# Recurrent mixer: the receptance's mixed tokens take the key's places tile by tile, and the systems leave by the inverse's places

## The chip, the cores and the metric

The kernel runs on one core of a Trainium2 chip as a single program. A core has a matrix engine (TensorE, in the rows PE, with its weight loads as PEld), a vector engine (VectorE, DVE), a scalar engine (ScalarE, ACT), a general engine (GpSimd, POOL) and a queue of transfers (SyncE, SP). Each works off its own list of instructions in order and waits for the others by semaphores. The metric is the device time of one execution in microseconds (us); the median of three runs before the change is 2302.98 us.

## The reference

Two layers, each a feed-forward network, a mixer, and a feed-forward network. The second mixer, which the change touches, is a recurrent one over 512 tokens with 16 heads of width 64:

```python
xx = jnp.pad(u, ((0, 0), (1, 0), (0, 0)))[:, :-1] - u

def proj(i):
    return (u + xx * mu[i]) @ w_in[:, int(offs[i]):int(offs[i + 1])]

r, k, v = proj(0), proj(1), proj(2)
...
def step(state, inp):
    r_t, w_t, k_t, v_t, kk_t, a_t = inp
    sa = jnp.einsum('bhvk,bhk->bhv', state, -kk_t)
    state = (state * w_t[:, :, None, :] + sa[..., None] * (kk_t * a_t)[:, :, None, :]
             + v_t[..., None] * k_t[:, :, None, :])
    return state, jnp.einsum('bhvk,bhk->bhv', state, r_t)
```

Receptance r, key k and value v are products of 1024 x 1024 with token-mixed copies of the input u. The recurrence is computed in chunks of 64 tokens; per head and chunk a triangular 64 x 64 system has to be inverted.

## The kernel before, in words

All of this is in `rwkv`. A product is done by `dense(i, off, evict, eng, ...)`: 8 tiles of 128 features, two halves g of four output banks each, and per tile and bank three matmuls of 128 x 512 (high and low parts of both operands, `mm3`, L195), so 192 for a product. In the first half the mixed tile `kt` is made by `mix` (L832 to L841): ScalarE scales u into a place of the tag `tb` (L837), VectorE adds the shifted u (L838), ScalarE rounds it to the high part in a place of the tag `big` (L839), and `eng` subtracts for the low part (L840). `tb` has two places, `big` eight, which is one product's tiles.

Around the products:

- `key` evicts the key's banks (L970 to L976: squares on ScalarE, a product with the decays, and the two sides A and B in the large tiles `ab`); its squares are summed by matmuls (L972).
- `root` (L982 to L984) makes the reciprocal norms, `normalise` spreads them by a matmul (L992) and VectorE scales A and B (L995). `systems(g, th)` multiplies B by A per head and chunk (L1010), VectorE masks the result (L1012) into a place of `tb`, and SyncE writes it to memory as md (L1013). g is the half of the heads, th the half of the chunks.
- `corners` (L1027, L1029) and `blocks(th)` (L1035 to L1045) read md back; `blocks` inverts 32 x 32 blocks by forward substitution on GpSimd: 31 steps of two dependent operations, 62 in all, in tiles of the tag `two`, which has four places. It carries a high priority. There is one inverse for each th.
- `receive` (L1094) folds r into A, `bonus` (L1102, L1104) sums r times k, `value` (L1117, L1119, L1120) parks v in memory.
- `convert` and `double` (L1059 to L1089) turn an inverse of 32 x 32 blocks into one of 64 x 64: a copy on ScalarE, transfers through memory (td), two rounds of 128 small matmuls (L1081, L1083) and evictions. The first is placed in the value's product, the second in the recurrence.
- `run` is the recurrence: 16 cycles u, in an order written out by hand. From cycle 1 on it multiplies by the first inverse (L1190), in each cycle GpSimd takes powers for the group norm (L1232) and products with the bonus (L1245), and VectorE scales by those powers one cycle later (L1235).

The order of instructions on each engine is set by a scheduler outside `run`: it takes instructions as they are written, moves them forward where they would be ready, and prefers those of high priority. On the chip each list is then fixed.

Of the kernel before, what the change touches and what calls it, by code (L numbers as in the profile page):

```python
# [9 lines left out]
F32 = mybir.dt.float32  # L10
# [6 lines left out]
P = 128  # L17
S = 512
# [14 lines left out]
C = 64  # L33
# [16 lines left out]
def weave(first, *others, every=1):  # L50

    for i, _ in enumerate(first):
        for g in others:
            if i % every == 0:
                next(g, None)
# [14 lines left out]
class Net:  # L70
# [711 lines left out]
    def rwkv(self, u, layer):  # L782
        nc, io = self.nc, self.io
# [48 lines left out]
        def mix(i, kt, eng):  # L832

            t = big()
            h, l = halves(t)
            x = vp.tile([P, S], F32, tag="tb", name="tb", bufs=2)
            nc.scalar.activation(x, u[:, kt, :], AF.Copy, scale=omu(i, kt))  # L837
            nc.vector.scalar_tensor_tensor(x[:, 1:], u[:, kt, 0:S - 1], mu(i, kt), x[:, 1:], op0=OP.mult, op1=OP.add)  # L838
            nc.scalar.activation(h, x, AF.Copy)  # L839
            eng.tensor_sub(l, x, h.bitcast(F32))  # L840
            return h, l  # L841
# [66 lines left out]
        def decays():  # L908

            kap = self.small([P, 2], "kap", 1)  # L910
            last = sides(KT - 1)[1][:, NC - 1, 2 * C - 1:]
            for i, k in enumerate((KAPPA, -KAPPA)):
                nc.vector.tensor_scalar(kap[:, i:i + 1], last, 0.0, k, op0=OP.mult, op1=OP.add)
                for g in gs:
                    n = g.shape[0]
                    nc.vector.scalar_tensor_tensor(kap[0:n, i:i + 1], g, 0.0, kap[0:n, i:i + 1], op0=OP.mult, op1=OP.add)
            for j in range(KT):
                A, B = sides(j)
                nc.scalar.activation(A[:, :, C:], v3(cums[j]), AF.Exp, scale=kap[:, 1:2])
                nc.scalar.activation(cums[j], cums[j], AF.Exp, scale=kap[:, 0:1])  # L920
                nc.scalar.activation(A[:, :, 0:C], B[:, :, C:], AF.Identity, scale=par(KA, j), bias=par(OKA, j))
                nc.gpsimd.tensor_copy(pc[:, j, :], A[:, :, 2 * C - 1])
                yield
# [6 lines left out]
                raws[n] = self.raw_weights()  # L930
            return raws.pop(n)

        def dense(i, off, evict, eng, other=iter(()), done=None):

            xs = {}
            for g in range(2):
                acc = [self.bank() for _ in range(4)]
                for kp in range(KT // 2):
                    w = self.weights(raw=load(off + 4 * g + kp))
                    anchor["act"], anchor["sp"] = self.last_hi, self.last_raw  # L940
                    for kk in range(2):
                        kt = 2 * kp + kk
                        if g == 0:
                            xs[kt] = mix(i, kt, eng())
                        for n in range(4):
                            ns, ws = slice(P * n, P * n + P), slice(512 * kk + P * n, 512 * kk + P * n + P)
                            if i == 2:
                                lhs, rhs = [t[:, ns] for t in xs[kt]], [t[:, 512 * kk:512 * kk + 512] for t in w[1:]]
                            else:
                                lhs, rhs = [t[:, ws] for t in w[1:]], xs[kt]  # L950
                            anchor["pe"] = self.mm3(acc[n], lhs, rhs, kt == 0, kt == KT - 1)
                        next(other, None)
                        yield
                for n in range(4):
                    evict(g, n, acc[n])
                    yield
                if done:
                    yield from done(g)
# [42 lines left out]
        def systems(g, th):  # L1001

            mask = tri[:, 0:C].rearrange("p (o t) -> p o t", o=1).to_broadcast([P, 2 * HC, C])
            for jp in range(2 * g, 2 * g + 2):
                gb = self.bank("ot").rearrange("p (q t) -> p q t", t=C)
                for q in range(2 * HC):
                    A, B = sides(2 * jp + q // HC)
                    c = HC * th + q % HC
                    for e in range(2):
                        nc.tensor.matmul(gb[own[e], q, :], B[own[e], c, 0:C], A[own[e], c, 0:C], start=True, stop=True)  # L1010
                gs = vp.tile([P, 2 * HC, C], F32, tag="tb", name="tb", bufs=2)
                nc.vector.tensor_tensor(gs, gb, mask, op=OP.mult)  # L1012
                nc.sync.dma_start(out=md[th][8 * jp:8 * jp + 8].rearrange("q e s t -> (e s) q t"), in_=gs)  # L1013
                yield
# [306 lines left out]
        def steps(*gs):  # L1321
            for g in gs:
                yield from g
# [11 lines left out]
                yield from normalise(0, 0, NC)  # L1335
                yield from steps(systems(0, 0), systems(0, 1))

        weave(steps(dense(1, 5, key, vec, decays(), heads_of)))
        for th in range(2):
            root(1, slice(HS * th, HS * th + HS))  # L1340
            weave(normalise(1, HC * th, HC))
            weave(systems(1, th))
            corners(th)
        weave(blocks(0))
        weave(blocks(1))
        weave(dense(0, 13, receive, vec))
        weave(bonus())
        fill = dense(2, 21, value, vec)
        for _ in range(9):
# [248 lines left out]
```

## Time and profile before

| what | us |
|---|---|
| median of three runs | 2302.98 (2302.13 to 2304.86) |
| the profiled execution | 2306.49 |
| its span, first to last instruction | 2304.6 |
| TensorE busy | 2190.6 (95%) |
| VectorE busy | 1527.2 (66%) |
| ScalarE busy | 1159.3 (50%) |
| GpSimd busy | 363.9 (16%) |

All later times are of the profiled execution, in us from the start of its span. Busy time counts what an engine executes; a busy TensorE is not one at its peak, since matmuls overlap, and its clock has two levels, shown as a share of the upper one. The recurrent mixer lies between about 1500 and 1930: the key's second half ends near 1603, the receptance's product runs from 1651 to the start of the value's, and the recurrence ends near 1860.

### The profile page before, as it was taken

To read this page: it belongs to the slowest core of one execution; us is meant where nothing else is said; L and a number is where in the kernel's file an instruction comes from. 1 tells how busy PE (TensorE), PEld (TensorE's weight loads), DVE (VectorE), ACT (ScalarE), POOL (GpSimd) and SP (SyncE) were. 2 spreads that over 40 slices of the span, in tenths; PEclk is the share of its full clock that TensorE was granted. 3 is DMA by queue.
4 is the path that set the end of the run, shared out by engine and by line. 5 is a ranking of instruction groups with operands and counts; after the bars stand their busy time and mean duration, and the time that the engine had idled before them with its cause. 6 is when DMAs were issued, how large, how long until landed. Compare 5 with 4: busy or idle time off the path is not lost.

```text
span 2304.6 us, 38449 instructions
## 1 busy us (share of the span) xinstructions
PE 2190.6 (95%) x15398; PEld 1921.0 (83%) x15398; DVE 1527.2 (66%) x2447; ACT 1159.3 (50%) x2282; POOL 363.9 (16%) x372
## 2 busy tenths in 40 slices
PE   7999999999999999999999999988699989899998
PEld 7999888877666889998799998866587867899987
DVE  8888625346777688872588874386663556888733
ACT  5555514465665455552445554286333754555532
POOL 4000004023100310000130000012493423100000
PEclk9999999999989999999999999999798989999999
DMA  4333333211001323333323333232443124333331
GB/s 174 101 104 111 101 95 109 83 46 46 29 1 65 101 83 110 107 94 102 110 83 100 103 101 108 85 104 92 75 114 122 47 83 162 94 109 99 96 107 67
DMA packets 93283, 214.33 MB, mean 93 GB/s; under 512 B 40752, under 2 KB 41392, under 8 KB 93104
## 3 DMA queue, kind: packets, MB, share of 16 engines
q1 hardware_dynamic: 93104, 211.88, 29.6%
q8 instruction: 121, 1.98, 0.4%
q14 instruction: 58, 0.48, 0.1%
HBM read 196.84 MB, written 15.01 MB: 92 GB/s over the span
## 4 chain that ended last, share of the span: by engine, by line
issue 29%; PE 24%; DVE 5%; POOL 4%; ACT 3%; DMA 1%; SPq 0%; DVEq 0%; POOLq 0%; ACTq 0%
PE p L195 19%; POOL two L1045 1%; POOL tmpi L1043 1%; PE p L1154 1%; ACT junk L218 1%; POOL sp L347 1%; PE p L1178 0%; DVE slot L201 0%; PE p L1170 0%; DVE xl L201 0%; DVE h L261 0%; PE p L972 0%; PE p L862 0%; PE p L1206 0%; PE p L1199 0%
## 5 line engine op out<-in xcount | busy, mean ns | idle before, releaser
L195 PE MATMUL p<-xh,whi 128*128 128x256 f32 (+1 forms) x1640 | 479.4, 296 | 18.3 <-ACT xh L200 8.4
L195 PE MATMUL p<-xl,whi 128*128 128x256 f32 (+1 forms) x1640 | 477.4, 294 | 3.4 <-DVE xl L201 3.4
L195 PE MATMUL p<-xh,wlo 128*128 128x256 f32 (+1 forms) x1640 | 457.9, 294 | 1.4 <-DVE wlo L201 1.4
L174 DVE TENSOR_TENSOR wlo<-raw,whi 128x1024 fp32r<-128x1024 f32 x150 | 190.2, 1269 | 316.7 <-ACT whi L170 316.7
L195 PE MATMUL p<-whi,slot 128*128 128x512 f32 x1280 | 395.1, 389 | 0.0
L195 PE MATMUL p<-slot,whi 128*128 128x256 f32 x1920 | 361.1, 284 | 12.5 <-issue 6.0
L170 ACT ACTIVATE whi<-raw 128x1024 fp32r<-128x1024 f32 x166 | 174.8, 1056 | 339.8 <-PE p L195 314.9
L195 PEld LDWEIGHTS p<-xh,whi 128*128 128x128 f32 x1640 | 319.1, 195 | 29.2 <-ACT xh L200 9.8
L195 PEld LDWEIGHTS p<-xl,whi 128*128 128x128 f32 x1640 | 320.2, 195 | 9.0 <-DVE xl L201 4.7
L195 PEld LDWEIGHTS p<-slot,whi 128*128 128x128 f32 x1920 | 303.4, 193 | 14.9 <-issue 6.2
L195 PEld LDWEIGHTS p<-xh,wlo 128*128 128x128 f32 x1640 | 309.5, 195 | 6.8 <-DVE wlo L201 1.6
L200 ACT ACTIVATE whi<-xn 128x1024 fp32r<-128x1024 f32 (+1 forms) x240 | 220.0, 917 | 184.7 <-PE p L195 133.8
L201 DVE TENSOR_TENSOR wlo<-xn,whi 128x1024 fp32r<-128x1024 f32 (+1 forms) x240 | 255.8, 1067 | 50.1 <-ACT whi L200 47.0
L195 PEld LDWEIGHTS p<-whi,slot 128*128 128x128 f32 x1280 | 240.0, 188 | 49.7
L195 PE MATMUL p<-slot,wlo 128*128 128x256 f32 x960 | 270.1, 284 | 0.0
L195 PE MATMUL p<-wlo,slot 128*128 128x512 f32 x640 | 249.0, 389 | 0.0
L222 POOL TENSOR_TENSOR rstd<-rstd,mhalf 128x1 f32<-128x1 f32 x48 | 30.1, 628 | 1348.0 <-DVE rstd L221 1347.2
L195 PEld LDWEIGHTS p<-slot,wlo 128*128 128x128 f32 x960 | 184.5, 193 | 0.0
L391 ACT ACTIVATE sp<-p 128x256 f32<-128x256 f32 x320 | 121.2, 379 | 112.6 <-PE p L195 112.6
L195 PEld LDWEIGHTS p<-wlo,slot 128*128 128x128 f32 x640 | 120.1, 188 | 24.9
L195 PE MATMUL p<-big,whi 128*128 128x512 f32 (+1 forms) x288 | 94.9, 412 | 12.0 <-ACT big L839 11.2
L200 ACT ACTIVATE whi<-raw 128x1024 fp32r<-128x1024 f32 x80 | 84.1, 1051 | 40.1 <-PE p L195 40.1
(321 smaller groups left out, 3754.1 us busy)
## 6 DMA issues: line engine op xcount, KB each, us to landing
raw<-in_wpack SPq DMA_DIRECT2D x252, 512.0 KB, 3.6
xn<-in_wpack SPq DMA_DIRECT2D x80, 512.0 KB, 3.5
hpark<-h SPq DMA_DIRECT2D x8, 512.0 KB, 2.7
h<-hpark SPq DMA_DIRECT2D x8, 512.0 KB, 4.7
h<-in_x SPq DMA_DIRECT2D x4, 512.0 KB, 7.1
gpost<-in_ffn_norm_post SPq DMA_DIRECT2D x4, 512.0 KB, 6.6
md<-tb SPq DMA_DIRECT2D x8, 256.0 KB, 2.8
td<-two SPq DMA_DIRECT2D x4, 512.0 KB, 2.8
```

The costliest lines, as they stand in the source:

```text
L170: self.last_hi = nc.scalar.activation(hi, raw, AF.Copy)
L174: (eng or nc.vector).tensor_sub(lo, raw, hi.bitcast(F32))
L195: m = self.nc.tensor.matmul(out, lhs[a], rhs[b], start=start and i == 0, stop=stop and i == 2, skip_group_check=more)
L200: i = self.nc.scalar.activation(hi, src, AF.Copy)
L201: return i, (eng or self.nc.vector).tensor_sub(lo, src, hi.bitcast(F32))
L218: nc.scalar.activation(self.junk(), src[q], AF.Square, scale=1.0 / (half * math.sqrt(D)), accum_out=ss[:, q:q + 1])
L222: nc.gpsimd.tensor_tensor(r[:, 1:2], r[:, 0:1], self.mhalf[:, 0:1], op=OP.pow)
L347: nc.gpsimd.tensor_sub(t4, q(xh, 1, 0, b), t2)
L391: copy = lambda dst, bank: nc.scalar.activation(dst, bank[:, 0:H], AF.Copy)
L1043: nc.gpsimd.tensor_tensor(t, ms[:, j, j + 1:32].rearrange("p (i o) -> p i o", o=1).to_broadcast([P, n, m]), T[:, j:j + 1, 0:m].to_broadcas ...
L1045: nc.gpsimd.tensor_tensor(T[:, j + 1:32, 0:m], T[:, j + 1:32, 0:m], t, op=OP.subtract)
L1154: nc.tensor.matmul(gb[e][:, j * P:j * P + P], B[own[e], j, c, :], A[own[e], j, c, :], start=True, stop=True)
```

## The change

Three edits. The receptance's mix of a tile is called right after the key's second half is done with the same tile (`then`), into the place of `big` that the key's tile leaves, and its subtraction goes to GpSimd instead of VectorE. The receptance's product no longer mixes; it takes the tiles that it is given. The masked systems are written from a place of `two` and no longer of `tb`, and the first inverse stands before the second half of the chunks' systems, so that each th is followed by its own inverse.

```diff
-        def dense(i, off, evict, eng, other=iter(()), done=None):
-
-            xs = {}
+        def dense(i, off, evict, eng, other=iter(()), done=None, xs=None, then=None):
+
+            xs = xs or {}
...
-                        if g == 0:
+                        if g == 0 and kt not in xs:
                             xs[kt] = mix(i, kt, eng())
...
                         next(other, None)
+                        if g and then:
+                            then(kt)
                         yield
...
-                gs = vp.tile([P, 2 * HC, C], F32, tag="tb", name="tb", bufs=2)
+                gs = two()[:, 0:S].rearrange("p (q t) -> p q t", t=C)
                 nc.vector.tensor_tensor(gs, gb, mask, op=OP.mult)
...
-        weave(steps(dense(1, 5, key, vec, decays(), heads_of)))
+        mixed = {}
+
+        def early(kt):
+
+            mixed[kt] = mix(0, kt, nc.gpsimd)
+
+        weave(steps(dense(1, 5, key, vec, decays(), heads_of, then=early)))
+        reads = dense(0, 13, receive, vec, xs=mixed)
         for th in range(2):
             root(1, slice(HS * th, HS * th + HS))
             weave(normalise(1, HC * th, HC))
             weave(systems(1, th))
             corners(th)
-        weave(blocks(0))
-        weave(blocks(1))
-        weave(dense(0, 13, receive, vec))
+            weave(blocks(th))
+        weave(reads)
         weave(bonus())
```

In the changed kernel the lines from L974 on are two further down: L992 becomes L994, L1010 L1012, L1012 L1014, L1043 L1045 and so on; the text below uses the old numbers except in the lists of the changed kernel.

TensorE before, after the key's product: p_16012 and p_16032 are the systems of the first chunks that the first inverse waits for, p_16082 and p_16102 those of the second chunks, p_16328 is the receptance's first bank.

```order
L992 MATMUL p_16008<-rinv,two 128x256
L1010 MATMUL p_16012<-ab 64x64 x16
L1010 MATMUL p_16032<-ab 64x64 x16
L992 MATMUL p_16066<-rinv,two 128x256
L992 MATMUL p_16070<-rinv,two 128x256
L992 MATMUL p_16074<-rinv,two 128x256
L992 MATMUL p_16078<-rinv,two 128x256
L1010 MATMUL p_16082<-ab 64x64 x16
L1010 MATMUL p_16102<-ab 64x64 x16
L195 MATMUL p_16328<-big,whi 128x512
L195 MATMUL p_16329<-big,whi 128x512
```

All systems stood ahead of the receptance. TensorE now, just after the key's last bank: p_16376 and p_16377 are the receptance's first two banks, L994 is the first half of heads being normalised.

```order
L195 MATMUL p_16377<-big,whi 128x512
L195 MATMUL p_16376<-big,wlo 128x512
L195 MATMUL p_16377<-big,wlo 128x512
L195 MATMUL p_16376<-big,whi 128x512 x2
L195 MATMUL p_16376<-big,wlo 128x512
L195 MATMUL p_16377<-big,whi 128x512 x2
L195 MATMUL p_16377<-big,wlo 128x512
L994 MATMUL p_15733<-rinv,two 128x512
L994 MATMUL p_15737<-rinv,two 128x512
L195 MATMUL p_16376<-big,whi 128x512
L195 MATMUL p_16377<-big,whi 128x512
```

The receptance starts before the first norm is spread and encloses these steps. TensorE now, in the value's first half (banks p_16689 to p_16692): p_16060 and p_16080 are the first chunks' systems, which before stood as p_16012 and p_16032.

```order
L195 MATMUL p_16691<-whi,big 128x512
L195 MATMUL p_16691<-wlo,big 128x512
L195 MATMUL p_16691<-whi,big 128x512
L1012 MATMUL p_16060<-ab 64x64 x16
L1012 MATMUL p_16080<-ab 64x64 x16
L195 MATMUL p_16692<-whi,big 128x512
L195 MATMUL p_16692<-wlo,big 128x512
```

The systems that open the first inverse have moved behind all 192 matmuls of the receptance and 18 of the value. GpSimd before, from the key's last eviction to the first inverse (L1043, L1045):

```order
L974 TENSOR_TENSOR ab<-tmp,ab 128x8x64 x2
L1029 MEMSET xl 32x16x32 x2
L974 TENSOR_TENSOR ab<-tmp,ab 128x8x64 x2
L1029 MEMSET xl 32x16x32 x2
L1037 MEMSET two 128x1024
L1038 MEMSET two 128x32
L1043 TENSOR_TENSOR tmpi<-two 128x31
L1045 TENSOR_TENSOR two<-two,tmpi 128x31
```

GpSimd now, the same stretch; L840 is the receptance's subtraction:

```order
L840 TENSOR_TENSOR big<-tb,big 128x512
L976 TENSOR_TENSOR ab<-tmp,ab 128x8x64
L840 TENSOR_TENSOR big<-tb,big 128x512 x2
L976 TENSOR_TENSOR ab<-tmp,ab 128x8x64
L840 TENSOR_TENSOR big<-tb,big 128x512 x2
L1031 MEMSET xl 32x16x32 x2
L1137 MEMSET xh 64x3072
L1039 MEMSET two 128x1024
L1040 MEMSET two 128x32
L1045 TENSOR_TENSOR tmpi<-two 128x31
L1047 TENSOR_TENSOR two<-two,tmpi 128x31
```

Eight subtractions stand between the key's evictions, and the clearing of xh (the place of u, for the recurrence), which stood inside the second inverse, has come ahead of the first.

## Rows read from the trace of the kernel before

**Rows 1.** Stretches: length, then busy PE, PEld, DVE, ACT, POOL; clock, DMA, GB/s.

```profile
1603.00:1651.00 48.00, 24.03 (x276) 16.07 (x276) 31.75 (x53) 6.62 (x14) 8.68 (x17) 0.69 0.45 96
...
1647.90:1704.70 56.80, 53.65 (x240) 43.83 (x240) 50.46 (x53) 28.21 (x39) 52.14 (x64) 0.94 0.26 64
...
1704.70:1749.10 44.40, 42.72 (x421) 35.28 (x422) 12.37 (x18) 14.24 (x18) 39.58 (x63) 0.92 0.44 114
```

**Rows 2.** TensorE's waits, 1603 to 1651: us in total, times, longest.

```profile
PE p L992 <- DVE rinv L201: 4.8, 1, 4.8
...
PE p L992 <- DVE ab L995: 4.7, 5, 2.8
```

**Rows 3.** TensorE by time: start, us, instruction, count, idle before.

```profile
1602.85 0.73 PE L992 MATMUL p<-rinv,two 64*128 64x512 f32 x2
...
1651.05 2.50 PE L195 MATMUL p<-big,whi 128*128 128x512 f32 x5 [7.10 <-ACT big L839]
...
1716.92 0.62 PE L195 MATMUL p<-whi,big 128*128 128x512 f32 x2
...
1732.32 0.39 PE L195 MATMUL p<-whi,big 128*128 128x512 f32 x1
...
1759.41 0.39 PE L195 MATMUL p<-whi,big 128*128 128x512 f32 x1
...
1778.54 0.68 PE L1190 MATMUL p<-xh,xl 64*64 64x64 f32 x16
```

**Rows 4.** The chain of waits from 1620 to 1648: start, us, what.

```profile
1620.70 5.33 PE p L972 x8
...
1633.58 3.69 PE p L1010 x64
...
1642.22 5.50 DMA two<-md
```

**Rows 5.** ScalarE by time: the receptance's first mixed tile.

```profile
1648.73 0.72 ACT L837 ACTIVATE tb<-xh,prm 128x512 f32<-128x512 f32 x1 [18.00 <-DMA md<-tb]
```

**Rows 6.** VectorE by time: the second mask of md0, and a later scaling.

```profile
1637.29 0.69 DVE L1012 TENSOR_TENSOR tb<-p,tri 128x512 f32<-128x512 f32 x1 [1.01 <-PE p L1010]
...
1792.59 0.42 DVE L1235 TENSOR_TENSOR big<-big,gr 128x256 f32<-128x256 f32 x1
```

**Rows 7.** GpSimd by time: ends of both inverses, and what follows.

```profile
1647.88 0.24 POOL L1043 TENSOR_TENSOR tmpi<-two 128x31 f32<-128x31 f32 x1 [22.45 <-DMA two<-md]
...
1704.42 0.25 POOL L1045 TENSOR_TENSOR two<-two,tmpi 128x31 f32<-128x31 f32 x1
...
1720.55 2.66 POOL L1135 MEMSET xh<- 64x3072 f32 x1
...
1748.77 0.25 POOL L1045 TENSOR_TENSOR two<-two,tmpi 128x31 f32<-128x31 f32 x1
...
1787.32 1.04 POOL L1232 TENSOR_TENSOR gr<-gv,mhalf 128x4 f32<-128x4 f32 x1 [12.42 <-DVE gv L1230]
```

**Rows 8.** Groups by shape: two of GpSimd, one of VectorE.

```profile
L201 POOL TENSOR_TENSOR xl<-sp,xh 128x512 fp32r<-128x512 f32 x8 | 16.8, 2110 | 6.0 <-ACT xh L200 6.0
...
L974 POOL TENSOR_TENSOR ab<-tmp,ab 128x512 f32<-128x512 f32 x7 | 10.4, 1480 | 30.7 <-DVE ab L973 30.6
...
L174 DVE TENSOR_TENSOR wlo<-raw,whi 128x1024 fp32r<-128x1024 f32 x150 | 190.2, 1269 | 316.7 <-ACT whi L170 316.7
```

**Rows 9.** Tile tb: duration min/median/max in ns, first and last start.

```profile
L838 DVE SCALAR_TENSOR_TENSOR tb<-xh,prm,tb x32: 723/751/1183, 1516.9 to 1699.2; 128x511 f32<-128x511 f32 x32
...
L840 DVE TENSOR_TENSOR big<-tb,big x32: 622/694/1124, 1518.4 to 1707.3; 128x512 fp32r<-128x512 f32 x32
```

**Rows 10.** VectorE's groups by shape, 1560 to 1711.

```profile
L995 DVE TENSOR_TENSOR ab<-ab,p 128x512 f32<-128x512 f32 x8 | 4.9, 672 | 0.0
```

**Rows 11.** SyncE's queue by time, after the first inverse.

```profile
1713.76 5.08 SPq L1069 DMA_DIRECT2D xl<-td  x8
...
1762.26 1.40 SPq L1120 DMA_DIRECT2D vpark<-tmp  x3
```

## The prediction

> **What bounds the kernel now.** I first read the chain that ended last: it runs through TensorE, and the page gives TensorE 95% of the span, so a gain must come from a stretch where TensorE stands idle. The stretches by window show the one that the change touches: from 1603, the key's end, to 1651, the receptance's start, TensorE is busy for 24.03 of 48.00 us at a granted clock of 0.69 of the upper level, and in the next, of 56.80 us, for 53.65 at 0.94 [rows 1]. Its waits name the cause: VectorE's reciprocal norms and its scaling of A and B [rows 2], a chain of small steps between engines. The last 7.10 us before the receptance go to ScalarE's first mixed tile [rows 3], and ScalarE itself had waited 18.00 us for a place of `tb`, until the masked system in it was written to md [rows 5]. The chain of waits passes the same points: the key's sums, 64 small matmuls, and the transfer back from md [rows 4].
>
> GpSimd comes next, since the inverses are its own. It waits 22.45 us for md, starts the first inverse at 1647.88, ends it at 1704.67 and ends the second at 1749.02 [rows 7]. TensorE does receptance and value in that time, until 1759.80, and first multiplies by an inverse at 1778.54 [rows 3]. So before, both inverses lie beside products that TensorE does anyway. Whether that stays so is the question.
>
> **The change part by part.** *Early mixing.* The receptance's 192 matmuls can begin at 1603. Between 1716.92 and 1732.32 the trace has 66 of the same shape in 15.40 us, 0.233 each [rows 3], so the product is 44.8 us, about what the gap is long. TensorE alone would then end the value some 40 us sooner. No work is removed: eight scalings, additions and roundings move forward, and eight subtractions go from VectorE to GpSimd.
>
> *The order on TensorE.* The systems that open the first inverse now stand behind the 192 matmuls of the receptance and 18 of the value. From 1602.85, TensorE has ahead of them: 210 × 0.233 = 49.0; the first half's 128 small matmuls, twice the row's 3.69 = 7.4; the key's sums, 5.33 at the low clock and, scaled from 0.69 to 0.92, about 4.0 [rows 1, 4]; eight spreading matmuls, from 0.73 for two [rows 3], about 2.2. That is 62.6. The systems themselves are another 3.7. For waits I add 5: a mixed tile takes 0.72 on ScalarE [rows 5], 0.75 on VectorE [rows 9], 0.72 again and 2.11 on GpSimd, 4.3 together; with two places of `tb` one tile comes every 2.1 us, while TensorE's first half uses one in 12 × 0.233 = 2.8 but can wait at its start and at the norms. The last system then ends near 1674.2 and its mask, 0.7 long [rows 6], near 1674.9. Before, from the end of that mask, 1637.98, to GpSimd's first step was 9.9 us of transfers [rows 6, 7]. The first inverse so starts at about 1685, 37 us later than before.
>
> VectorE's list in the same stretch is no shorter: 12 roundings of weights at 1.27 [rows 8], 14 mixing additions at 0.75 [rows 9], and 62 others at about 0.67 [rows 10], 67 us. It has no slack to catch up with, which is why I add 5 and not 0.
>
> *The subtraction on GpSimd.* The trace has no such instruction. Below, it costs nothing where GpSimd keeps up. From above the nearest rows are a GpSimd subtraction with the same output type, 2110 ns, and a product of the same size, 1480 [rows 8]; VectorE's own is 0.694 [rows 9]. I take 2.11: eight make 16.9 us on an engine that was busy 8.68 in 48 us [rows 1]. They are hidden unless its four products for the key's B fall due behind them; those wait for 2 × 2.11 at most, and the norms of the second half wait for them.
>
> *Systems in a place of `two`.* This ends the 18.00 us wait [rows 5]. Late next are then the two places of `tb` among the mixed tiles themselves and the order above. SyncE's writes of md stand behind loads of raw weights, which wait for VectorE; this is within the 9.9 if VectorE is not late, up to 5 more if it is.
>
> *The inverses.* Each is 62 dependent steps with TensorE not involved. Before, the first took 56.8 with VectorE busy 50.46 of 56.80; the second took 44.35, 2.66 of it clearing xh, with VectorE busy 12.37 of 44.40 [rows 1, 7]. So a step costs 0.92 beside a busy VectorE and 0.67 beside an idle one, both engines being stretched: VectorE's subtraction has 0.694 as median and 1.124 as longest [rows 9]. Now both run later, from 1685, mostly beside the value's product, and the second is followed by none of VectorE's mixing. I take 46 for each, the second with six products for the bonus on GpSimd among its steps. Ends: 1731 and 1777. The clearing of xh has moved ahead of the first, where GpSimd waits anyway.
>
> *What follows.* From the end of the first inverse to the transfers of its conversion was 1704.67 to 1718.84, 14.2 us [rows 7, 11]; the second part, from the last of the value's parking transfers ahead of the doubling, 1762.26, to the recurrence's first use, 16.3 [rows 3, 11]. Before, the recurrence waited for the value and not for the inverse. Now its first use is at 1731 + 14.2 + 16.3 = 1761.5, 17.0 us earlier than 1778.54. But GpSimd owes VectorE the powers for the group norm: VectorE used them at 1792.59 and GpSimd had made them from 1787.32 [rows 6, 7]. They stand behind the second inverse, so they come at 1777 + 1.0 = 1778, where the earlier recurrence wants them at 1792.59 − 17.0 = 1775.6. That takes 2.4 back, and 14.5 remain.
>
> **Sum.** The profiled execution took 2306.49, 1.9 more than its span and 3.5 above the median of the runs. 2306.5 − 14.5 = 2292.0; against the median, 2302.98 − 14.5 = 2288.5. Each us by which the inverses start later costs one: no gain is left at a start of about 1699.5.
>
> **The shared port.** VectorE and GpSimd were both busy for nearly all of the 56.80 us of the first inverse, 50.46 and 52.14 [rows 1]; if each instruction shut the other engine out, the two sums could not lie in 56.80 us, though both were stretched. The Trainium skill, SBUF — State Buffer, section "Who interferes with whom", has the port pair that these two engines share as an exclusive lock, held for a whole instruction. By that rule the times of rival C would hold; by the rows the overlap is partial, and the trace agrees with the rule only in the stretching.
>
> **Rivals.**
>
> A, the forecast: the gap is filled, the inverses become the bound, a gain of 4.6 to 25. The best corner: a start at 1680 with 88 for both inverses, 44 as the second before, gives 23 or so. Chance 0.70.
>
> B, the inverses stay hidden, and all 40 us of TensorE arrive: near 2260. It needs a start of the first inverse close to 1648, thus the systems ahead of most of the receptance on the chip, against the fixed order. Chance 0.06.
>
> C, slower: GpSimd's eight subtractions and four products hold VectorE up for their full length, 8 × 2.11 + 4 × 1.48 = 22.8 us on top of a list with no slack. The first inverse then starts near 1697 (half of it hidden in waits), takes 56.6 beside the delayed VectorE, and the second ends near 1799. The powers come at 1800, 7.3 us after 1792.59: about 2310. It decides from where the start and both durations together pass 1791.5, which is 1792.59 less the 1.04 of the powers. For it speak the overlapped stretch above; against it that GpSimd's records before lie close beside VectorE's. Chance 0.12.
>
> D, no change, because the later start eats just what the filled gap gives: a start between 1695 and 1704 with inverses of 46. Same end, about 2303. Chance 0.12.
>
> **How the numbers follow.** What a measurement of this kernel can tell from no change is about 0.2%, 4.6 us. Faster by more than that: A and B, 0.76; within it: D, 0.12; slower: C, 0.12. The range goes from the best corner with a few us for faster waits, 2278, to D's upper part, 2304; B and C lie outside and are 0.18.
>
> **What would show it.** Right after 1603 TensorE should have the receptance (before: 1651), with the granted clock at 0.9 or more up to the value. GpSimd's subtraction should read 1.5 to 2.1 us. Its first inverse should start at 1685, 1675 to 1697 with the other theories, and end at 1731, the second at 1777; the recurrence's first product with an inverse should stand near 1761 with a wait for the inverse's doubling ahead of it, and VectorE should wait for the powers by 2 us or so. The value's last matmul should lie near 1720, and TensorE idle after it. The forecast is wrong if the first inverse takes over 55 us, or if it starts after 1700; and if it starts before 1660, B holds.

## The result, and the profile after

The changed kernel took 2285.8 us (median of 4 runs, 2284.43 to 2286.36), the kernel before 2302.56 in the same comparison (4 runs). The ratio is 0.9926, 95% interval 0.9911 to 0.9941: 17 us faster, where 14.5 had been forecast. A second comparison of the same two gave 0.9933 (0.9913 to 0.9953).

The profiled execution shows the chain that was forecast, with each point within eleven us of its place. The stretches by window of the changed kernel (length, busy PE, PEld, DVE, ACT, POOL, clock, DMA, GB/s), which answer to [rows 1]:

```profile
1603.00:1651.00 48.00, 44.56 (x274) 31.65 (x274) 39.79 (x52) 19.12 (x31) 15.87 (x13) 0.93 0.40 109
1680.00:1731.00 51.00, 51.00 (x280) 42.40 (x278) 17.99 (x28) 11.10 (x12) 42.40 (x75) 0.87 0.53 143
1731.00:1777.00 46.00, 37.40 (x783) 32.79 (x784) 18.50 (x37) 19.82 (x66) 38.23 (x65) 0.83 0.39 98
```

The gap is filled: TensorE is busy 44.56 of the 48 us, at a clock of 0.93 instead of 0.69. The idle time has moved to 1731 and later, where TensorE now has the recurrence to wait for. TensorE by time (start, us, instruction, count, idle before), which answers to [rows 3]:

```profile
1636.78 3.62 PE L974 MATMUL p<-tmp,ind 128*32 128x512 f32 x8
...
1670.01 2.08 PE L1012 MATMUL p<-ab 64*64 64x64 f32 x64
...
1730.24 0.39 PE L195 MATMUL p<-whi,big 128*128 128x512 f32 x1
...
1731.86 0.32 PE L1083 MATMUL p<-two,xl 32*32 32x32 f32 x4 [0.79 <-DMA two<-td]
...
1751.61 0.68 PE L1192 MATMUL p<-xh,xl 64*64 64x64 f32 x16
...
1774.66 1.07 PE L1180 MATMUL p<-xh,big 128*64 128x64 f32 x16 [4.99 <-DVE tmp L1218]
```

The systems of the first chunks stand at 1670 (before 1633.58), the value's last matmul at 1730.24 (before 1759.41), and the first inverse is used at 1751.61 (before 1778.54). Then comes a new wait of 4.99 us in the second cycle. GpSimd's rows and VectorE's say why ([rows 6, 7] before):

```profile
1609.80 2.19 POOL L840 TENSOR_TENSOR big<-tb,big 128x512 fp32r<-128x512 f32 x1
...
1683.12 0.24 POOL L1045 TENSOR_TENSOR tmpi<-two 128x31 f32<-128x31 f32 x1 [7.15 <-DMA two<-md]
...
1725.03 0.25 POOL L1047 TENSOR_TENSOR two<-two,tmpi 128x31 f32<-128x31 f32 x1
...
1770.62 0.25 POOL L1047 TENSOR_TENSOR two<-two,tmpi 128x31 f32<-128x31 f32 x1
1770.83 1.04 POOL L1234 TENSOR_TENSOR gr<-gv,mhalf 128x4 f32<-128x4 f32 x1
```

```profile
1771.90 0.42 DVE L1237 TENSOR_TENSOR big<-big,gr 128x256 f32<-128x256 f32 x1 [6.10 <-POOL gr L1234]
```

The inverses run from 1683.12 to 1725.28 and to 1770.87, back to back, and the powers (L1234) follow directly behind the second. VectorE had waited 6.10 us for them. In the chain that ended last, the stretch from the key's last sums to the first inverse now reads:

```profile
1636.85 3.55 PE p L974 x8
1640.40 14.72 PE p L195 x62
...
1655.54 7.69 PE p L195 x32
...
1670.08 1.10 PE p L1012 x32
...
1673.13 2.61 DMA md<-two
```

It goes through the receptance's large matmuls (L195): the systems wait for their turn in TensorE's list.

**A measure for the experiments.** In the later comparisons the kernel before took 2294 to 2311 us from run to run, so small differences between kernels are read from the profiles, as the stretch from the key's first sums to the recurrence's end (the first transposes of the last part). Its two ends, in the changed kernel:

```profile
1583.49 1.05 PE L974 MATMUL p<-tmp,ind 128*32 128x512 f32 x2
...
1846.29 1.08 PE L1308 MATMUL p<-ident,big 128*128 128x128 f32 x4 [0.94 <-ACT two L1258]
```

That is 262.8 us. Before it was 285.0:

```profile
1582.25 1.04 PE L972 MATMUL p<-tmp,ind 128*32 128x512 f32 x2
...
1867.23 1.08 PE L1306 MATMUL p<-ident,big 128*128 128x128 f32 x4 [0.94 <-ACT two L1256]
```

All points of the table count from the key's first sums:

| kernel | first inverse starts | first, second inverse end | value ends | first use | stretch | ratio to before (95%) |
|---|---|---|---|---|---|---|
| before | 65.6 | 122.4, 166.8 | 177.6 | 196.3 | 285.0 | 1 |
| changed | 99.6 | 141.8, 187.4 | 147.1 | 168.1 | 262.8 | 0.9926 (0.9911 to 0.9941) |
| changed, again | 99.0 | 141.0, 186.5 | 146.8 | 164.8 | 261.9 | 0.9933 (0.9913 to 0.9953) |
| gs_two | 109.3 | 153.8, 193.3 | 146.0 | 178.0 | 267.0 | 0.9889 (0.9870 to 0.9908) |
| gs_tb | 83.0 | 133.9, 175.9 | 173.1 | 184.5 | 273.8 | 0.9919 (0.9896 to 0.9941) |
| delay | 102.6 | 149.3, 190.0 | 146.9 | 177.5 | 265.6 | 0.9896 (0.9874 to 0.9918) |
| inv_order | 114.4 | 160.9, 197.8 | 146.9 | 184.2 | 272.0 | 0.9949 (0.9930 to 0.9969) |
| inv_split | 99.2 | 141.5, 197.2 | 146.8 | 167.7 | 261.3 | 0.9894 (0.9873 to 0.9914) |
| short | 99.9 | 141.8, – | 147.0 | 168.4 | 256.2 | 0.9866 (0.9845 to 0.9887) |
| sub_vector | 93.8 | 136.6, 185.5 | 149.9 | 163.7 | 254.7 | 0.9871 (0.9850 to 0.9892) |
| sub_vector, again | 93.8 | 136.5, 187.0 | 150.0 | 166.9 | 256.4 | 0.9875 (0.9856 to 0.9893) |
| sub_split | 93.5 | 136.4, 192.6 | 149.6 | 164.1 | 257.7 | 0.9892 (0.9872 to 0.9913) |
| sub_split4 | 93.8 | 136.6, 189.7 | 150.0 | 164.6 | 254.7 | 0.9893 (0.9871 to 0.9915) |
| sub_pin | 83.5 | 131.5, 174.3 | 169.0 | 186.4 | 274.7 | 0.9962 (0.9948 to 0.9975) |

Two profiles of one kernel differ by 0.9 and 1.7 in the stretch. The ratio also holds the 2000 us around it, and its order is not always the stretch's: the two profiles of the changed kernel reach the key's first sums at 1583.49 and at 1576.67, so some 7 us of difference can lie ahead of the stretch alone. gs_two, gs_tb, delay and inv_order have their profiles from executions 7 to 13 us above their medians. By the ratio gs_two and delay are faster than the changed kernel, by the stretch slower; that difference stays open.

### The profile page after: what moved, and what is told of

The parts are those of the page before. It is cut to its first block, busy times and chain, and to the rows that moved or that the text cites. A ratio compares the mean times of both kernels' runs of the same rounds, so it can differ in the third digit from the quotient of the medians.

```text
span 2284.3 us, 38446 instructions
## 1 busy us (share of the span) xinstructions
PE 2189.8 (96%) x15398; PEld 1921.1 (84%) x15398; DVE 1514.3 (66%) x2439; ACT 1157.7 (51%) x2282; POOL 358.0 (16%) x380
## 4 chain that ended last, share of the span: by engine, by line
issue 29%; PE 23%; DVE 5%; POOL 4%; ACT 3%; DMA 1%; SPq 0%; POOLq 0%; DVEq 0%; ACTq 0%
PE p L195 19%; POOL two L1047 1%; POOL tmpi L1045 1%; ACT junk L218 1%; POOL sp L347 1%; PE p L1156 1%; DVE slot L201 1%; DVE xl L201 0%; DVE h L261 0%; DVE wlo L174 0%; POOL rstd L222 0%; PE p L862 0%; PE p L974 0%; PE p L1317 0%; PE p L1172 0%
## 5 line engine op out<-in xcount | busy, mean ns | idle before, releaser
L195 PE MATMUL p<-xh,whi 128*128 128x256 f32 (+1 forms) x1640 | 480.6, 297 | 19.4 <-ACT xh L200 8.4
L195 PE MATMUL p<-xl,whi 128*128 128x256 f32 (+1 forms) x1640 | 478.8, 295 | 3.4 <-DVE xl L201 3.3
L195 PE MATMUL p<-xh,wlo 128*128 128x256 f32 (+1 forms) x1640 | 458.9, 295 | 0.3 <-DVE wlo L201 0.3
L195 PE MATMUL p<-whi,slot 128*128 128x512 f32 x1280 | 395.1, 390 | 0.0
L195 PE MATMUL p<-slot,whi 128*128 128x256 f32 x1920 | 363.1, 286 | 11.3 <-issue 6.0
L195 PEld LDWEIGHTS p<-xh,whi 128*128 128x128 f32 x1640 | 320.5, 196 | 30.3 <-ACT xh L200 9.8
L195 PEld LDWEIGHTS p<-xl,whi 128*128 128x128 f32 x1640 | 321.5, 196 | 9.0 <-DVE xl L201 4.7
L195 PEld LDWEIGHTS p<-slot,whi 128*128 128x128 f32 x1920 | 305.3, 194 | 13.4 <-issue 6.2
L195 PEld LDWEIGHTS p<-xh,wlo 128*128 128x128 f32 x1640 | 310.3, 196 | 5.7 <-DVE wlo L201 0.5
L195 PEld LDWEIGHTS p<-whi,slot 128*128 128x128 f32 x1280 | 240.1, 188 | 49.5
L195 PE MATMUL p<-slot,wlo 128*128 128x256 f32 x960 | 271.1, 285 | 0.0
L195 PE MATMUL p<-wlo,slot 128*128 128x512 f32 x640 | 249.2, 389 | 0.0
L195 PEld LDWEIGHTS p<-slot,wlo 128*128 128x128 f32 x960 | 185.7, 194 | 0.0
L195 PEld LDWEIGHTS p<-wlo,slot 128*128 128x128 f32 x640 | 120.2, 188 | 24.9
L195 PE MATMUL p<-big,whi 128*128 128x512 f32 (+1 forms) x288 | 97.1, 416 | 7.8 <-ACT big L839 5.3
```

Of the source, the lines that this page charges most:

```text
L195: m = self.nc.tensor.matmul(out, lhs[a], rhs[b], start=start and i == 0, stop=stop and i == 2, skip_group_check=more)
```

## The experiments

**One edit alone: the masked systems in a place of `two`** (gs_two).

```diff
-                gs = vp.tile([P, 2 * HC, C], F32, tag="tb", name="tb", bufs=2)
+                gs = two()[:, 0:S].rearrange("p (q t) -> p q t", t=C)
```

> The kernel before with one of the three edits alone: the masked systems are written from a place of `two`; the receptance still mixes inside its own product, on VectorE. Theory A (the early calls of the mix fill the gap, as the prediction's working has it; the other place only ends the 18.00 us wait): the receptance starts at most 7.1 us sooner, and the time is 2296 to 2302. Theory B (the place of `tb` was all that kept the scheduler from issuing the receptance into the gap; written later, it is moved forward anyway): in this kernel's list on TensorE 217 of the receptance's and value's matmuls already stand between the key's last sums and the first systems of the first chunks, 245 in the changed kernel; so the first inverse starts at 1677 to 1683 and the time is 2280 to 2288, as the changed kernel's 2285.8.

The ratio is 0.9889, 25.6 below the kernel before (2278.76, just under the theory's 2280 to 2288), so theory B: the wait for the place of `tb` alone had kept the receptance out of the gap. Freed of it, the scheduler moved the product forward although it is written later, and the value ends at 146.0, as in the changed kernel. The start of the first inverse was missed: 109.3 instead of 93 to 99. GpSimd's rows of this kernel give the reason:

```profile
1681.00 0.96 POOL L1037 MEMSET two<- 128x1024 f32 x1 [10.35 <-PE p L992]
...
1693.44 0.61 POOL L1043 TENSOR_TENSOR tmpi<-two 128x31 f32<-128x31 f32 x1 [11.26 <-DMA two<-md]
```

Its tile waits for TensorE's last spreading matmuls, which read from a place of `two`, and its transfer comes late.

**The order of the inverses undone** (inv_order).

```diff
             corners(th)
-            weave(blocks(th))
+        weave(blocks(0))
+        weave(blocks(1))
         weave(reads)
```

> The changed kernel with the third edit undone: both chunks' systems are written ahead of both inverses. In its lists nothing moves on TensorE. Theory places (the inverse's three tiles come from the four places of `two`, and now stand behind the masked systems of the second chunks, which are written from such places): the first inverse starts 10 to 17 us later, at 110 to 117 us after the key's first sums, and as the inverses set the end, the time is 7 to 17 us above the changed kernel's in the same comparison. Rival (the order in which they are written is without effect, as TensorE's list is the same): within 3 us.

The start comes at 114.4, inside the 110 to 117 of the theory of places: the order in which tiles are written decides who gets the four places of `two`, though TensorE's list is the same. TensorE's longest wait:

```profile
PE p L1083 <- DMA two<-td: 15.9, 2, 15.4
```

It is now for the first inverse. The stretch grew by 9 to 10 us; the median, 2288.98 beside 2286.65, by 2.3 and not by the 7 to 17 of the theory, in runs that spread by ten and more, which cannot settle it.

**One edit undone: the masked systems back in `tb`** (gs_tb).

```diff
-                gs = two()[:, 0:S].rearrange("p (q t) -> p q t", t=C)
+                gs = vp.tile([P, 2 * HC, C], F32, tag="tb", name="tb", bufs=2)
```

> The changed kernel with one edit undone: the masked systems go back to a place of `tb`. In its list on TensorE only 130 of the large matmuls stand ahead of the first chunks' systems instead of 245, and one round of the first inverse's doubling stands inside the value's product again. Theory chain (the time follows the start of GpSimd's first inverse, one for one, until TensorE's own work decides): 115 x 0.233 = 27 us less ahead of the systems, a start near 1656 to 1665, both inverses done by 1755, no wait for the powers, and then TensorE decides: 2272 to 2280. Rival (the places of `tb` that wait for their writes to md stall the mix and so TensorE, as the 18.00 us wait before): 2290 or more.

Neither theory. The first inverse starts 16.6 sooner, the powers cost no wait, and yet the stretch is 11 longer than the changed kernel's. The gap by window (columns as above), and TensorE's longest wait (us in total, times, longest):

```profile
1603.00:1651.00 48.00, 36.47 (x236) 24.27 (x235) 40.62 (x51) 18.16 (x31) 17.87 (x15) 0.89 0.32 83
```

```profile
PE p L1083 <- DMA two<-td: 8.4, 1, 8.4
```

TensorE is idle for 11.5 us of the gap, mostly in waits for VectorE's scaling and masks, and for 8.4 more inside the value's product, where the doubling now stands. The value ends at 173.1, and from there on TensorE decides. This profile is of the kernel's slowest run, 2297.49 where the median is 2284.88; by the ratio, 0.9919, the kernel is level with the changed one.

**The first inverse later** (delay).

```diff
+            if th == 0:
+                for _ in range(10):
+                    nc.gpsimd.memset(T.rearrange("p i k -> p (i k)")[:, 0:1024], 0.0)
+                nc.gpsimd.memset(T.rearrange("p i k -> p (i k)")[:, 0:1024:33], 1.0)
```

> The changed kernel with ten more clearings of the first inverse's tile (128 x 1024, 0.95 us each in the changed kernel) and one more of 0.17 on GpSimd ahead of its first step, 9.7 us. Theory chain (the inverses set the end): 9.7 later one for one, 2294 to 2297. Rival (TensorE's work decides, and the inverses are mostly hidden): 2286 to 2289.

The dose was smaller than meant. GpSimd by time:

```profile
1678.37 10.05 POOL L1043 MEMSET two<- 128x1024 f32 x10
...
1688.73 0.24 POOL L1049 TENSOR_TENSOR tmpi<-two 128x31 f32<-128x31 f32 x1
```

Most of the 10 us lie in the 7.15 that GpSimd would have waited for md, and the start moved by only 3.0. The second inverse ended 2.6 later and the stretch grew by 2.8, but the second inverse is not the reason: the first, stretched from 42.2 to 46.7 us, ended 7.5 later, the first use came 9.3 later, and VectorE no longer waits for the powers. TensorE's wait for the first inverse's transfers, and VectorE at the first powers:

```profile
PE p L1087 <- DMA two<-td: 6.4, 2, 5.7
```

```profile
1777.84 0.41 DVE L1241 TENSOR_TENSOR big<-big,gr 128x256 f32<-128x256 f32 x1
```

Neither time came: the median, 2281.07, lies below both ranges, and the ratio, 0.9896, shows no loss at all.

**The powers ahead of the second inverse's end** (inv_split).

```diff
-            weave(blocks(th))
+            late = blocks(th)
+            for _ in range(31 - 8 * th):
+                next(late)
...
+                    for _ in range({2: 3, 3: 3, 4: 3}.get(u, 0)):
+                        next(late, None)
                     if u == 5:
```

> The changed kernel with the last 8 of the second inverse's 31 steps moved into the recurrence's cycles 2, 3 and 4 (three, three and two), behind the powers of each cycle. Theory powers (what holds TensorE for 5.0 us and VectorE for 6.1 in the second cycle is that GpSimd makes the powers only after the second inverse): the wait goes, and the time is 4 to 6 us below the changed kernel's in the same comparison. Rival (the second inverse then ends about 10 us later, and the wait comes back at its doubling in cycles 7 and 8): 0 to 2 below.

The powers come 6.7 sooner (VectorE uses them at 181.7 instead of 188.4), but the stretch is only 0.6 to 1.5 shorter. Most of the wait has moved, as the rival said, though to another engine. ScalarE by time:

```profile
1772.52 1.94 ACT L1061 ACTIVATE two<-two 128x1024 f32<-128x1024 f32 x1 [3.45 <-POOL two L1047]
```

ScalarE copies the second inverse in cycle 5 and holds up the recurrence's own copies behind it; TensorE's longest wait for those is 4.9. The time, in the median 10.8 us below the changed kernel's, is better than the profile has it and than the 4 to 6 of the theory; which of the two is right stays open.

**The second inverse cut short** (short).

```diff
-            for j in range(31):
+            for j in range(31 - 15 * th):
```

> The changed kernel without the last 15 of the second inverse's 31 steps (that part of the inverse is left out of the computation). Theory powers (the powers that stand behind the second inverse hold the recurrence for 5 to 7 us, and nothing else of that inverse does): from the key's first sums to the recurrence's end 255 to 258 us, where the changed kernel has 262, and a ratio of 0.990 to 0.991 to the kernel before. Rival (the two inverses delay the recurrence at no place that counts): 261 to 263.

256.2, within the 255 to 258 of the theory: that wait is worth 6 us, and the second inverse costs the changed kernel nothing else. It is the clean form of what inv_split tried. The ratio, 0.9866, went further than the 0.990 to 0.991 expected.

**The subtraction on VectorE** (sub_vector; again as sub_again).

```diff
-            mixed[kt] = mix(0, kt, nc.gpsimd)
+            mixed[kt] = mix(0, kt, nc.vector)
```

> The changed kernel with the receptance's subtraction on VectorE instead of GpSimd. Theory chain: 8 x 0.69 = 5.6 us more on a VectorE list without slack, the first inverse up to 5.6 later, 2286 to 2291. Rival (the two engines hold each other up, and GpSimd's eight subtractions of 1.3 to 2.2 us cost VectorE or the mix more than they save): the start comes 5 or more sooner, and the time is 2278 to 2283. In its list 217 large matmuls stand ahead of the first chunks' systems, 245 in the changed kernel, which speaks for the rival.

> The kernel with the receptance's subtraction on VectorE once more, as the reference of this comparison: a ratio of 0.985 to 0.989 to the kernel before; 254 to 256 us from the key's first sums to the recurrence's end in the profile.

The rival holds, with times below its 2278 to 2283: 2274.84 and 2275.07 in the two comparisons, ratios 0.9871 and 0.9875, the lowest of the complete kernels. The subtraction's durations (min/median/max, ns) in the changed kernel on GpSimd and in sub_vector on VectorE:

```profile
L840 POOL TENSOR_TENSOR big<-tb,big x8: 1282/1512/2185, 1596.3 to 1626.5; 128x512 fp32r<-128x512 f32 x8
```

```profile
L840 DVE TENSOR_TENSOR big<-tb,big x16: 666/682/692, 1593.2 to 1666.5; 128x512 fp32r<-128x512 f32 x16
```

A mixed tile is ready 0.8 us sooner on VectorE, and TensorE's waits for GpSimd's subtraction (1.7 in the changed kernel) are gone. With the shorter mix the scheduler also put 28 fewer large matmuls ahead of the systems, 28 × 0.233 = 6.5 us, and the first inverse starts 5.8 sooner. It also put the first powers ahead of the inverse's last steps, so that VectorE has them at 182.1, before the inverse ends at 185.5.

**Both together** (sub_split, and with 4 steps instead of 8, in cycles 2 and 3, sub_split4).

> The receptance's subtraction on VectorE, and the second inverse's last 8 steps in the recurrence's cycles 2 to 4: the two changes that by the runs so far take GpSimd's inverse off the end. If both are independent, sub_vector's 30.8 below the kernel before and its remaining wait of 3.2: 33 to 36 us below the kernel before in the same comparison, a ratio of 0.985 to 0.986. Rival (sub_vector's start is early enough, TensorE's own work decides): as sub_vector, a ratio of 0.987.

> The subtraction on VectorE and only the last 4 steps of the second inverse moved into cycles 2 and 3 (8 steps into cycles 2 to 4 gave 257.7 from the key's first sums to the recurrence's end, 254.7 without). Theory balance (ScalarE copies the second inverse at the end of cycle 5, and 8 moved steps, with their ten us of other work between them, end behind that): with 4 the inverse ends in time, the wait of 3.2 for the powers goes, and the stretch is 251 to 253. Rival (GpSimd's work in these cycles is as long as they are, and each step moved comes back as a wait): 255 to 258.

Nothing is added: 257.7 and 254.7 beside 254.7 and 256.4, ratios 0.9892 and 0.9893. So no gain, as both rivals had it, though sub_split's ratio is above its 0.987 and sub_split4's stretch just under its 255. What is moved returns: in sub_split TensorE waits up to 4.0 us for ScalarE's copies, as in inv_split, and in sub_split4 VectorE still waits 2.9 for the powers.

**The systems ahead of the receptance's second half** (sub_pin).

```diff
+                        pinned[g, th] = nc.tensor.matmul(gb[own[e], q, :], B[own[e], c, 0:C], A[own[e], c, 0:C], start=True, stop=True)
...
-        weave(reads)
+        for _ in range(12):
+            next(reads)
+        with self.tc.issue_after(pinned[1, 0].ins):
+            weave(reads)
```

> The subtraction on VectorE, and the second half of the receptance's matmuls pinned behind the first chunks' systems on TensorE, so that 84 large matmuls stand between the first norm and those systems instead of 170. Theory chain (the start of the first inverse still sets the end): it starts 15 to 20 us sooner, near 75 to 79 us after the key's first sums, and the stretch from there to the recurrence's end falls from 254.7 by the powers' wait and more, to 245 to 251. Rival (with the subtraction on VectorE, TensorE's own list decides: the pinned matmuls leave it idle between the norms, and the doubling that returns into the value's product moves the value's end): the inverse does start that much sooner, but the stretch is 255 to 265.

The rival again, and clearly: the first inverse starts 10 sooner than in sub_vector (not 15 to 20), and the stretch is 18 to 20 longer, 274.7, beyond the rival's 265. TensorE's waits:

```profile
PE p L994 <- DVE ab L997: 7.4, 3, 4.4
PE p L1085 <- DMA two<-td: 5.8, 2, 4.8
PE p L1182 <- DMA xh<-vpark: 5.5, 1, 5.5
```

The wait for the norms is back, the doubling stands inside the value's product again, and behind the value TensorE waits for parked values to return.

## Why the prediction was right, point by point

**The gap is filled: right.** Granted clock 0.93 and 3.4 us idle instead of 24. TensorE's part was over-estimated: the value ended at 1730.63, not near 1720, so that 30.4 of the 40 us came. From the key's first sums to the value's end, before and after (columns as above):

```profile
1582.25:1759.80 177.55, 151.85 (x1059) 116.93 (x1059) 110.07 (x139) 57.22 (x83) 105.47 (x144) 0.88 0.38 97
```

```profile
1583.49:1730.63 147.14, 143.70 (x795) 108.28 (x795) 94.98 (x131) 51.67 (x75) 71.12 (x100) 0.93 0.41 111
```

Idle time fell from 25.70 to 3.44 us, and busy time by 8.15, about 4 of it the first inverse's doubling, which now stands behind the value. The 40 us took most of the gap's 48 for gain, though TensorE was busy in 24.03 of them and that work is still to be done.

**Which edit does it: not as told.** The prediction gave the gain to the early mixing and let the other place end a wait of 18.00. The runs show that the other place alone brings the receptance forward as far as all three edits (gs_two: the value ends at 146.0), and the early call and the new order without it only in part (gs_tb: TensorE busy 36.47 of the 48 us, the value's end at 173.1). With its subtraction on GpSimd the early call costs: by the ratios sub_vector is some 13 us below the changed kernel (0.9871 and 0.9875 beside 0.9926 and 0.9933). Whether it gives anything at all is open. The systems of the first chunks in gs_two, which has no early call, and in sub_vector:

```profile
1664.64 2.08 PE L1010 MATMUL p<-ab 64*64 64x64 f32 x64
```

```profile
1657.95 2.08 PE L1012 MATMUL p<-ab 64*64 64x64 f32 x64
```

That is 80.5 and 80.1 us after the key's first sums, where the changed kernel has 86.5; gs_two's late first inverse comes from the place that it waits for. No run has the other place and the new order without the early call.

**The start of the first inverse: right.** 1683.12 beside 1685; the mask's end 1673.1 beside 1674.9, and 10.0 from there to the first step as worked out (9.9). TensorE stood idle for 3.4 us, where 5 had been put in for waits. The 5 had been argued from a list of 67 us on VectorE without slack; it had some, 59.34 us busy in 70:

```profile
1603.00:1673.00 70.00, 66.56 (x419) 48.60 (x419) 59.34 (x84) 29.07 (x45) 18.52 (x14) 0.95 0.38 106
```

**The inverses: right, one in size off.** 42.2 for the first (46 forecast), 45.6 for the second with its bonus products (46).

**From the first inverse to its use: off by four.** 26.3 from 1725.28 to 1751.61, where 30.5 had been carried over from before. There the parts were 14.2 to the end of the transfers and 16.3 from the parking transfers to the first use. The same transfers in the changed kernel, on SyncE's queue:

```profile
1730.68 4.95 SPq L1071 DMA_DIRECT2D xl<-td  x8
```

They end at 1735.63, so the first part took 10.4, and the rest 16.0. That the second term came out is luck: it was taken from a stretch with no doubling in it, since before both rounds (1732.64 and 1739.88) lay inside the value's product. Now both follow the value and take 7 us of a time in which the recurrence, in the kernel before, only started up. From the value's end to the first use it took 18.7 before, and 18.0 to 21.3 with both rounds in it (changed kernel, its repeat, inv_split, short). The changed kernel and its repeat:

```profile
1730.63:1751.61 20.98, 18.61 (x370) 16.26 (x367) 6.03 (x8) 8.31 (x15) 16.07 (x26) 0.67 0.70 166
```

```profile
1723.47:1741.47 18.00, 14.23 (x369) 12.21 (x367) 5.78 (x8) 8.31 (x14) 13.81 (x22) 0.91 0.81 189
```

The granted clock differs, 0.67 and 0.91, and nearly the same matmuls (370 and 369) took 18.61 and 14.23 us. In the changed kernel TensorE waits only 1.3 us for the first inverse's transfers (0.79 and 0.51): the first inverse and the value come out almost together, so that the first use is bound by the inverse as forecast, but barely.

**The powers: right.** Forecast to be late by 2.4; VectorE waits for them 6.10, since the recurrence came sooner. That the first use came ten us ahead of the forecast does not show in the time, as the powers stand behind the second inverse. The end of the second inverse, six us earlier than forecast, is the whole difference: 1792.59 to 1771.90 is 20.7 us, and the profiled execution is 20.3 shorter. The runs give 17, as the profiled execution before (2306.49) lay 3.9 above its median.

**That the inverses set the end: shown, by two routes.** The stretch ends 87.8 to 89.5 us behind the first use where VectorE waits at most 2.3 us for the powers and ScalarE's copy of the second inverse holds nothing up (before, gs_two, gs_tb, delay, inv_order, short, sub_again, sub_pin). It ends later by about the wait where VectorE waits longer: 90.1 for 2.93 (sub_split4), 91.0 for 4.29 (sub_vector), 94.7 for 6.10 (changed) and 97.1 for 8.59 (its repeat). So in the changed kernel the second inverse costs 6 to 9 us through the powers, and short, in which that wait is gone, has 256.2. In gs_two, delay and inv_order it is the other way round: TensorE waits up to 11.7, 5.7 and 15.4 us for the first inverse's transfers, and VectorE 2.0, 0 and 0.5 for the powers. The waits of gs_two, which delay and inv_order have above, and VectorE at the first powers in gs_two and in inv_order:

```profile
PE p L1081 <- DMA two<-td: 12.1, 2, 11.7
```

```profile
1778.42 0.42 DVE L1235 TENSOR_TENSOR big<-big,gr 128x256 f32<-128x256 f32 x1 [1.96 <-POOL gr L1232]
```

```profile
1785.75 0.43 DVE L1237 TENSOR_TENSOR big<-big,gr 128x256 f32<-128x256 f32 x1 [0.53 <-POOL gr L1234]
```

There the first inverse sets the end, through the first use. That the stretch ends 73.7 to 75.6 behind the second inverse in five kernels (those three, the changed kernel and its repeat) shows nothing by itself, as the two inverses stand back to back. In gs_tb, sub_pin and the kernel before, TensorE's own list decides: the stretch ends 101 to 107 behind the value. Even with the powers' wait gone (short) it is 29 shorter than before, so rival B's 40 were no possibility of this list, and the break-even of 1699.5, worked out for the start alone, was too simple, as a later first inverse also takes away the powers' wait: it leaves gs_two 7 us of gain for its start (109.3, which is 1692.8 in the changed kernel's profile) and inv_order 1.6 (1697.9), and their stretches are 18 and 13 shorter than before.

**Rival C: its mechanism exists, its size does not.** The prediction compared busy times, which was loose, as an instruction that is held up counts as busy. Two groups of VectorE beside GpSimd's first inverse, in the kernel before (us in total, mean ns), and the same in sub_vector without it:

```profile
L840 DVE TENSOR_TENSOR big<-tb,big 128x512 fp32r<-128x512 f32 x15 | 14.7, 1002 | 0.2 <-ACT big L839 0.2
...
L1094 DVE TENSOR_TENSOR ab<-ab,p 128x512 f32<-128x512 f32 x8 | 5.3, 678 | 1.2 <-PE p L195 1.2
```

```profile
L840 DVE TENSOR_TENSOR big<-tb,big 128x512 fp32r<-128x512 f32 x15 | 10.1, 680 | 0.2 <-ACT big L839 0.2
L1096 DVE TENSOR_TENSOR ab<-ab,p 128x512 f32<-128x512 f32 x8 | 5.0, 667 | 0.0
```

The subtraction, with both operands in SBUF, goes from 680 to 1002 ns; the product with one operand in PSUM stays at 667 to 678. The Trainium skill, SBUF — State Buffer, section "Who interferes with whom", says this: with two SBUF inputs VectorE contends with a GpSimd instruction that reads SBUF; with at most one, outside its two-port modes, it does not. The trace agrees in which instructions are stretched. Beside the eight subtractions of the changed kernel it shows in single instructions:

```profile
1605.07 2.19 DVE L174 TENSOR_TENSOR wlo<-raw,whi 128x1024 fp32r<-128x1024 f32 x1
...
1609.64 1.21 DVE L174 TENSOR_TENSOR wlo<-raw,whi 128x1024 fp32r<-128x1024 f32 x1
```

The first of these roundings of weights started behind a subtraction on GpSimd and took a microsecond more; the second started ahead of one and kept its length, and that subtraction (1609.80, above) took 2.19 instead of the 1.28 to 1.30 of the shortest four. VectorE lost some 2 us in this way on two of its roundings (the other, at 1598.81, took 2.06), not the 22.8 of rival C, and the first inverse took 42.2, not 56.6.

## What to carry to other kernels

Before a product is moved forward by hand, see what keeps the scheduler from doing it: here one place of a rotating tag, held by a slow write, and giving that writer another tag did the whole of it. When a filled gap makes room on the busiest engine, follow the longest serial chain that used to hide beside it, and write its end as an equation with the first consumer behind it; but work out the busy engine's own list as well, with every small matmul, since pulling the chain forward at its cost lost more than the chain gave (sub_pin by stretch and ratio, gs_tb by the stretch alone). Before a chain is held to set the end, look at the wait of each of its consumers: here it was the powers in some kernels and the first use in others. An engine that is mostly idle is no free place for work that sits on a chain: GpSimd took 1512 ns, in the median, for what VectorE did in 682.

## What the runs showed of the hardware that was not expected

GpSimd's steps beside VectorE are lengthened singly, not evenly: in the changed kernel a step on 128 x 207 elements took 0.60 us in the second inverse and 1.65 in the first, where a rounding of weights on VectorE had started just ahead of it.

```profile
1715.00 1.65 POOL L1047 TENSOR_TENSOR two<-two,tmpi 128x207 f32<-128x207 f32 x1
...
1735.58 0.60 POOL L1047 TENSOR_TENSOR two<-two,tmpi 128x207 f32<-128x207 f32 x1
```

```profile
1714.97 1.23 DVE L174 TENSOR_TENSOR wlo<-raw,whi 128x1024 fp32r<-128x1024 f32 x1 [4.61 <-ACT whi L170]
```

That is 1.05 more, nearly the length of that one VectorE instruction. Four of the 62 steps of that inverse took over 1.3 us; it lasted 42.2 us in all, against 56.8 in the kernel before, where VectorE was busy almost throughout.
